# The scale of a gate's weights: one four-column fp32 matmul, summed by the copying activation, in place of four one-column matmuls

## The chip, the core and the metric

The kernel runs on one core of a Trainium2 chip. Five engines work side by side, each through its own instructions in order: TensorE (PE, matmuls; its weight loads are listed as PEld), VectorE (DVE), ScalarE (ACT), GpSimd (POOL) and SyncE (SP, which issues the DMAs). An engine stops at an instruction whose inputs or buffers are not ready, and everything behind that instruction waits with it. The metric is device time in microseconds, the median of repeated runs. In the traces, f32 in a weight's or product's row stands for fp32 or for the 32-bit matmul type that the code calls F32R; a "hi" and a "lo" part are a value rounded to a shorter type and the remainder.

## What is computed

One layer of a hybrid encoder on 1024 tokens of width 1024: RMS norm, one input projection, attention and a gated MLP beside each other, a projection of each, a merge by two sigmoid gates, an output projection, residual and a last RMS norm. The part that matters here is the merge:

```
h = rmsnorm(x, norm_gain)
g_merge = h @ w_in[:, 2816:4864]                     # 2 x 1024 columns
g = sigmoid(g_merge.reshape(B, S, 2, 1024) + b_merge)
y = g[:, :, 0, :] * y_a + g[:, :, 1, :] * y_b
out = rmsnorm(x + y @ w_out, final_gain)
```

## The kernel before

Channels are handled in eight tiles of 128. After attention come these stages: eight projections of the MLP branch (tile `yb`, line 634, PSUM copied to `y` at line 635), then for each of the eight channel tiles a *pair* of gates (`g0` to `g7`), and between them the projections of the attention branch (`y`, lines 806 ff.), then the output projection (`out`).

The two gates of a channel tile are computed together by Strassen's scheme in Winograd's form: the products are named `11`, `21`, `T2`, `T3`, `T1`, `22` and `T4`, in this order, each of four times three matmuls (line 174: hi times hi, line 175: weight hi times data lo, line 176: weight lo times data hi), 84 matmuls in a pair. The weights of a pair are loaded raw (`graw`, lines 811 and 812, two transfers of 512 KB), combined into sums (`s1`, `s2`), and split into an fp16 hi part by ACT (line 682) and a lo part by DVE (line 683), into the tiles `wg..`; three buffers of these exist. The data side are the forms `xf..` of the normalised input, made once by DVE and ACT from `xraw` (lines 112, 118 and 650) around the last `yb` projections; the forms of the attention output (`gf..`, `gk`, from `gat`) are made on the same lines in the same place.

So that the fp16 parts stay in range, the weights of a pair are divided by the root of their mean square. `pair_weights` squares the four raw quarters on ACT, each with a sum per partition into one column of `ss` (line 816, tile `gss`). `unit_scale` then adds the four columns over all partitions by matmuls with a constant matrix (line 671, tile `usg`), copies the result (line 673), and makes the scale on POOL in four small operations (lines 674 to 677, tile `scg`); ACT and DVE need the result of line 675 for the hi and lo parts, and line 677's for the tanh.

Nothing in the source fixes the order on the engines. A scheduler with a time line of its own orders the instructions of each engine, and tiles are taken from pools when it has a buffer free: of the tag `qT` there are four of 8 KB per partition, which hold `gat0`, `gat2`, the `graw` tiles and the `ya` tiles in turn. The order of the steps is asked for by one line:

```
MORDER = "w0 g0 w1 g1 w2 A a0 g2 w3 g3 w4 a1 g4 w5 g5 w6 a2 g6 w7 a3 o g7"
```

`w` is `pair_weights`, `g` the pair of gates, `A` the forms of the attention output, `a` its projections.

Of the kernel before, what the change touches and what calls it, by code (L numbers as in the profile page):

```python
# [12 lines left out]
AF = mybir.ActivationFunctionType  # L13
# [3 lines left out]
P = 128  # L17
# [13 lines left out]
def hybrid_block_kernel(  # L31
# [11 lines left out]
    act, dve, pool, pe = nc.scalar, nc.vector, nc.gpsimd, nc.tensor  # L43
# [24 lines left out]
    def const(shape, name, dt=F32):  # L68
        return sb.tile(shape, dt, tag=name, bufs=1, name=name)
# [4 lines left out]
    def ps_o(name):  # L74
        return ps.tile([P, 512], F32, tag="o", bufs=1, name=name)

    def ps_z(name):
        return ps.tile([P, 512], F32, tag="z", bufs=1, name=name)

    def ps_oz(i, name):  # L80
        return (ps_z if i % 2 else ps_o)(name)
# [13 lines left out]
    mscale = const([P, 1], "mscale")  # L95
# [169 lines left out]
    for h in range(2):  # L265
        pt = ps_o(f"wsum{h}")
# [143 lines left out]
    pt = ps_o("vabT")  # L410
# [4 lines left out]
    pt = ps_z("vmxB")  # L415
# [18 lines left out]
    for t2k in range(4):  # L434
        pt = ps_oz(t2k, f"ktp{t2k}")
# [230 lines left out]
    def unit_scale(ss, n, name):  # L666

        nscale.append(name)
        pt = ps_oz(len(nscale), f"us{name}")
        for i in range(n):  # L670
            pe.matmul(pt[:, 0:1], mscale.broadcast_to([P, P]), ss[:, i:i + 1], start=(i == 0), stop=(i == n - 1))
        sc = sb.tile([P, 2], F32, tag="sc", bufs=3, name=f"sc{name}")
        act.copy(sc[:, 1:2], pt[:, 0:1])  # L673
        pool.tensor_scalar(out=sc[:, 1:2], in0=sc[:, 1:2], scalar1=1.0, scalar2=1e-30, op0=ALU.mult, op1=ALU.add)  # L674
        pool.tensor_tensor(out=sc[:, 0:1], in0=sc[:, 1:2], in1=mhalf[:, 0:1], op=ALU.pow)
        pool.tensor_tensor(out=sc[:, 1:2], in0=sc[:, 1:2], in1=sc[:, 0:1], op=ALU.mult)
        pool.tensor_scalar(out=sc[:, 1:2], in0=sc[:, 1:2], scalar1=gsc[:, 1:2], scalar2=1.0, op0=ALU.mult, op1=ALU.mult)
        return sc
# [130 lines left out]
    def pair_weights(dt):  # L809
        t = t8("qT", 4, f"graw{dt}", F32)  # L810
        nc.sync.dma_start(out=t[:, 0, :], in_=wall[W_TR + 20 + dt])
        nc.sync.dma_start(out=t[:, 1, :], in_=wall[W_TR + 12 + dt])
        a21, a22, a11, a12 = (t[:, k, H(h)] for k in range(2) for h in range(2))
        ss = small(f"gss{dt}", 4)
        for i, t in enumerate((a21, a22, a11, a12)):
            act.activation(junk(f"gsq{dt}{i}"), t, AF.Square, accum_out=ss[:, i:i + 1])
        sc = unit_scale(ss, 4, f"g{dt}")
        return sums(a11, a12, a21, a22, t2(f"s1{dt}"), t2(f"s2{dt}")), sc
# [65 lines left out]
    for step in MORDER.split():  # L884
        i = int(step[1:] or 0)
# [153 lines left out]
```

## Time and profile before

| | |
|---|---|
| median of 3 runs | 735.65 us (735.62 to 738.46) |
| the profiled execution | 736.99 us |
| its span, first to last instruction | 735.2 us |
| PE busy | 714.0 us (97%) |
| DVE busy | 565.9 us (77%) |
| ACT busy | 431.2 us (59%) |
| POOL busy | 110.4 us (15%) |
| mean granted TensorE clock | 0.992 |

The profiled execution is 1.3 us (0.2%) above the median; 1.8 us of it lie outside the span. In rows of a timeline the columns are start, duration (both us), engine, line, operation, output<-input tiles with buffer numbers left out, shape, count, and in brackets the idle time of the engine ahead of it with what ended it. Neighbouring instructions on one engine overlap a little, so their distance is shorter than a duration. The rows of the chain of waits give start, length and what the time was spent on. In the rows of a table by stretches of time, busy time and number of instructions are given for PE, PEld, DVE, ACT and POOL, then the granted TensorE clock (1.00 is full), the share of DMA and GB/s.

### The profile page before, as it was taken

The numbers are of one execution on the slowest core, as the hardware profiler recorded it, in microseconds if no ns is written. First come the engines' busy times: TensorE is split into PE (matmuls) and PEld (weight loads), VectorE is DVE, ScalarE is ACT, GpSimd is POOL, SyncE is SP. The second block draws the span as 40 slices with busy tenths as digits, with TensorE's granted clock in tenths as the row PEclk, the third lists the DMA queues.
The fourth block names the chain that finished last, engine by engine and source line by source line (L and its number), as shares of the span: only waits on it lengthen the run. The fifth ranks groups of instructions, "written<-read, shape, count | busy, mean of one in ns | idle before, by whom it ended". The sixth has DMA issues, their size and how long they took to land.

```text
span 735.2 us, 11836 instructions
## 1 busy us (share of the span) xinstructions
PE 714.0 (97%) x4633; PEld 531.4 (72%) x4633; DVE 565.9 (77%) x822; ACT 431.2 (59%) x770; POOL 110.4 (15%) x101
## 2 busy tenths in 40 slices
PE   8999999998999999999999996999999999999996
PEld 8978888776777788788887883465464556488885
DVE  6556868799797988878789999888887898952223
ACT  6634564685797887777784775654455536621011
POOL 0011223133132232213200003001101110000000
PEclk9999999999999999999999998999999999999999
DMA  8830301054889999998999500130121005440202
GB/s 307 317 129 1 115 16 43 1 122 94 150 157 182 176 180 167 183 170 175 154 245 287 132 30 14 45 129 15 46 98 58 0 1 184 157 146 1 114 30 86
DMA packets 152904, 85.59 MB, mean 116 GB/s; under 512 B 135440, under 2 KB 136080, under 8 KB 152848
## 3 DMA queue, kind: packets, MB, share of 16 engines
q1 hardware_dynamic: 152560, 84.56, 46.6%
q8 instruction: 36, 0.59, 0.3%
q10 hardware_dynamic: 288, 0.28, 0.1%
q14 instruction: 20, 0.16, 0.1%
HBM read 47.07 MB, written 4.19 MB: 70 GB/s over the span
## 4 chain that ended last, share of the span: by engine, by line
PE 83%; DVE 5%; ACT 5%; DMA 5%; issue 1%; POOL 1%; SPq 0%; POOLq 0%; ACTq 0%; DVEq 0%
PE o L576 5%; PE out L175 4%; DMA T<-p 4%; PE out L176 4%; PE out L174 4%; PE s L550 3%; PE s L551 3%; PE g L174 3%; PE g L175 3%; PE g L176 3%; PE gb L488 2%; PE q L174 2%; PE q L175 2%; PE v L175 2%; PE v L174 2%; PE q L176 2%
## 5 line engine op out<-in xcount | busy, mean ns | idle before, releaser
L564 DVE SCALAR_TENSOR_TENSOR p<-P,ri,p 128x1024 f16<-128x1024 f32 x64 | 83.4, 1304 | 26.4 <-ACT p L563 26.3
L557 ACT ACTIVATE P<-s,nm 128x1024 f32<-128x1024 f32 x64 | 71.2, 1113 | 24.2 <-DVE nm L553 20.8
L563 ACT ACTIVATE p<-P,ri 128x1024 f16<-128x1024 f32 x64 | 73.1, 1145 | 15.7 <-DMA T<-p 8.8
L553 DVE TENSOR_REDUCE nm<-s 128x1 f32<-128x1024 f32 x64 | 77.6, 1214 | 3.0 <-PE s L551 2.9
L576 PEld LDWEIGHTS <-vS 128*64 128x64 f16 x1536 | 45.3, 111 | 19.0 <-issue 17.8
L576 PE MATMUL o<-T,vS 128*64 128x128 f16 x1536 | 52.0, 222 | 4.2 <-DMA T<-p 3.8
L118 POOL TENSOR_TENSOR wl<-wraw,wh 128x512 fp32r<-128x512 f32 x24 | 39.9, 1665 | 97.7 <-ACT wh L112 55.6
L550 PE MATMUL s<-kT,qT 128*128 128x512 f32 x128 | 52.9, 413 | 0.0
L551 PE MATMUL s<-kT,qT 128*128 128x512 f32 x128 | 50.9, 397 | 0.0
L911 ACT ACTIVATE sq<-xr 128x1024 f32<-128x1024 f32 x7 | 7.4, 1062 | 65.4 <-DVE xr L969 65.4
L969 DVE TENSOR_TENSOR xr<-out,xr 128x1024 f32<-128x1024 f32 x7 | 8.6, 1224 | 47.6 <-PE out L176 47.5
L674 POOL TENSOR_SCALAR scg<-scg 128x1 f32<-128x1 f32 x8 | 6.5, 807 | 206.7 <-ACT scg L673 206.6
L550 PEld LDWEIGHTS s<-kT,qT 128*128 128x128 f32 x128 | 24.3, 189 | 6.3 <-issue 0.2
L551 PEld LDWEIGHTS s<-kT,qT 128*128 128x128 f32 x128 | 24.3, 190 | 5.4 <-issue 0.2
L112 ACT CAST wh<-wraw 128x512 fp32r<-128x512 f32 x35 | 21.4, 616 | 10.4 <-PE ga L489 3.4
L682 ACT ACTIVATE wg<-graw,scg 128x512 f16<-128x512 f32 x16 | 11.4, 721 | 26.6 <-PE g L176 13.2
L488 PE MATMUL ga<-xh,wh 128*128 128x512 f32 x64 | 26.0, 406 | 0.8 <-DVE ga30w L494 0.5
L488 PE MATMUL u<-xh,wh 128*128 128x512 f32 x64 | 25.8, 402 | 0.0
L488 PE MATMUL gb<-xh,wh 128*128 128x512 f32 x64 | 25.5, 399 | 0.0
L175 PE MATMUL yb<-gml,wh 128*128 128x512 f32 x64 | 25.5, 398 | 0.0
L490 PE MATMUL u<-xh,wl 128*128 128x512 f32 x64 | 25.4, 397 | 0.0
L490 PE MATMUL gb<-xh,wl 128*128 128x512 f32 x64 | 25.4, 396 | 0.0
(554 smaller groups left out, 2143.9 us busy)
## 6 DMA issues: line engine op xcount, KB each, us to landing
wraw<-in_wall_dram SPq DMA_DIRECT2D x59, 256.0 KB, 3.4
graw<-in_wall_dram SPq DMA_DIRECT2D x16, 512.0 KB, 5.8
xraw<-in_xT_dram SPq DMA_DIRECT2D x13, 512.0 KB, 6.4
xn<-in_x_dram SPq DMA_DIRECT2D x8, 512.0 KB, 6.3
wor<-in_wall_dram SPq DMA_DIRECT2D x8, 512.0 KB, 5.1
xr<-in_x_dram SPq DMA_DIRECT2D x8, 512.0 KB, 3.8
out_dram<-xr SPq DMA_DIRECT2D x7, 512.0 KB, 2.6
xraw<-in_xT_dram SPq DMA_DIRECT2D x5, 256.0 KB, 5.5
```

What stands on the lines that cost most here:

```text
L174: pe.matmul(o, ah, bh, start=start, stop=False)
L175: pe.matmul(o, ah, bl, start=False, stop=False)
L176: pe.matmul(o, al, bh, start=False, stop=stop)
L488: pe.matmul(o, wh[:, C(dt % 4)], xh[dt][:, H(h)], start=(dt == 0), stop=False)
L490: pe.matmul(o, wl[:, C(dt % 4)], xh[dt][:, H(h)], start=False, stop=(dt == 7))
L550: pe.matmul(sp[:, H(hf)], qs, kT[:, 2 * v, H(hf)], start=True, stop=False)
L551: pe.matmul(sp[:, H(hf)], qs, kT[:, 2 * v + 1, H(hf)], start=False, stop=True)
L553: dve.tensor_reduce(out=nm, in_=sp, axis=AX.X, op=ALU.max, negate=True)
L557: act.activation(Pt, sp, AF.Exp, bias=nm, accum_out=rsum)
L563: act.activation(hi, Pt, AF.Copy, scale=ri)
L564: dve.scalar_tensor_tensor(out=lo, in0=Pt, scalar=ri, in1=hi, op0=ALU.mult, op1=ALU.subtract)
L576: pe.matmul(ot[64 * h:64 * h + 64, 0:128], vS[:, kt, v, 64 * vl:64 * vl + 64], T[:, h, 8 * p + kt, :], start=(n == 0), stop=(n == len(part ...
```

## The change

Four matmuls of one column, each adding to the same PSUM column, become one matmul of four columns. The copy from PSUM becomes an activation that copies the four sums to an unused place of the same PSUM tile and adds them into the scale tile by its accumulator. The sum is the same; 24 of the 32 matmul instructions of the eight pairs go, and the eight activations each get an instruction that reads the accumulator.

```
 pt = ps_oz(len(nscale), f"us{name}")
-for i in range(n):
-    pe.matmul(pt[:, 0:1], mscale.broadcast_to([P, P]), ss[:, i:i + 1], start=(i == 0), stop=(i == n - 1))
+pe.matmul(pt[:, 0:n], mscale.broadcast_to([P, P]), ss[:, 0:n], start=True, stop=True)
 sc = sb.tile([P, 2], F32, tag="sc", bufs=3, name=f"sc{name}")
-act.copy(sc[:, 1:2], pt[:, 0:1])
+act.activation(pt[:, 8:8 + n], pt[:, 0:n], AF.Copy, accum_out=sc[:, 1:2])
```

The scheduler orders the program anew. Line numbers from 672 on are one lower in the changed kernel (its line 670 is the matmul, 672 the activation, 681 and 682 the hi and lo parts, 815 the squares); the text uses the numbers of before. Names in the rows below carry the pair's number and the product (`wg011` is the weight of pair 0, product 11) and a buffer number.

On ACT, around the first scale, before: the copies of the scales of pairs 0 and 1 stand behind the last `y` copy (`y47<-yb7`), and the first hi parts behind them.

```order
L635 COPY y47_5097<-yb7_5442 128x1024
L112 CAST gk_5829<-gat2_4640 128x1024
L673 COPY scg0_5491<-usg0_5486 128x1
L673 COPY scg1_5645<-usg1_5640 128x1
L112 CAST xfT33_5399<-xraw7_5229 128x512
L682 ACTIVATE wg011_5505<-graw0_5474,scg0_5491 128x512
L682 ACTIVATE wg021_5522<-graw0_5474,scg0_5491 128x512
```

On ACT, the same place after:

```order
L112 CAST gf110_5801<-gat0_2003 128x1024
L635 COPY y47_5097<-yb4_5321 128x1024
L112 CAST xf222_5305<-xraw2_5167 128x512
L672 ACTIVATE usg0_5486,scg0_5488<-usg0_5486 128x4
L112 CAST xfT40_5164<-xraw4_5104 128x512
L112 CAST xfT22_5312<-xraw6_5169 128x512
L112 CAST xfT42_5318<-xraw3_5227 128x512
L112 CAST xfT11_5210<-xraw1_5106 128x512
L112 CAST wp0011_5840<-wraw380_5831 128x256
L635 COPY y47_5097<-yb5_5353 128x1024
L681 ACTIVATE wg011_5502<-graw0_5474,scg0_5488 128x512
```

The scale of pair 0 has moved ahead by three `y` copies and stands in the middle of the making of the forms, and its first hi part stands two `y` copies ahead of the last. The cast `gf110` has moved behind the cast of the last MLP weights and so stands directly ahead of the copy of `yb4` and the cast of `xf222`.

On DVE, the stretch that leads to the first lo part, after; before, `wg011` stood 19 rows further down, behind the last of the forms of product 21.

```order
L118 TENSOR_TENSOR gf111_5802<-gat0_2003,gf110_5801 128x1024
L118 TENSOR_TENSOR xfT22_5312<-xraw6_5169,xfT22_5312 128x512
L118 TENSOR_TENSOR xfT42_5318<-xraw3_5227,xfT42_5318 128x512
L650 TENSOR_TENSOR xraw1_5106<-xraw5_5108,xraw1_5106 128x512
L118 TENSOR_TENSOR xfT11_5210<-xraw1_5106,xfT11_5210 128x512
L118 TENSOR_TENSOR wp0011_5840<-wraw380_5831,wp0011_5840 128x256
L650 TENSOR_TENSOR gat0_2003<-gat0_2003 128x2x512
L682 SCALAR_TENSOR_TENSOR wg011_5502<-graw0_5474,scg0_5488,wg011_5502 128x512
```

The same set of operations up to `wp0011` and the subtraction `gat0` stood there before; the lo part of pair 0 now follows them. Further down, up to the lo part of pair 0's product T4, DVE has three operations fewer ahead of it than before: the last subtraction on `gat2` (line 650), `gk` and `gfT31` (line 118) now stand behind it.

On PE, the scale of pair 2. Before, its four matmuls stood between matmuls of pair 0 (one in product T1, one in 22, two at the end of 22); here the last two:

```order
L176 LDWEIGHTS wg022_5592
L176 MATMUL g022_5595<-xfT13_5392,wg022_5592 128x512
L671 MATMUL usg2_5794<-gss2_5785,mscale_63 128x1 x2
L174 LDWEIGHTS wg0T4_5610
L174 MATMUL g0T4_5613<-xfT40_5164,wg0T4_5610 128x512
```

After, the only one stands between the end of pair 0 and pair 1:

```order
L176 LDWEIGHTS wg0T4_5607
L176 MATMUL g0T4_5610<-xf213_5404,wg0T4_5607 128x512
L670 MATMUL usg2_5788<-gss2_5779,mscale_63 128x4
L174 LDWEIGHTS wg111_5653
L174 MATMUL g111_5656<-xf110_5146,wg111_5653 128x512
```

It has moved behind the last product of pair 0. The buffers moved too: before, the raw weights of pair 2 (`graw2`) were put into the buffer that `gat0` leaves; in the changed program they get the buffer of `graw0`, whose last reader is the lo part of pair 0's product T4 on DVE. The rows of SP stand in the same order in both. The matmuls of the scales of pairs 3 to 7 stood before as three together and one alone (pairs 3, 5 and 7) or as four apart (4 and 6); now each pair has one.

## The prediction

> **What bounds the kernel now.** I read the page first, then who waits for whom on PE, the chain of waits around the longest such wait, and then each engine's instructions in order of time there.
>
> ```profile
> span 735.2 us, 11836 instructions
> PE 714.0 (97%) x4633; PEld 531.4 (72%) x4633; DVE 565.9 (77%) x822; ACT 431.2 (59%) x770; POOL 110.4 (15%) x101
> PE g L174 <- ACT wg L682: 6.2, 1, 6.2
> 443.73 0.94 ACT gk L112
> 444.83 3.56 POOL scg L674
> 448.75 0.57 POOL scg L675
> 449.34 0.73 ACT wg L682
> 450.11 0.61 PE g L174
> 451.15 0.43 PE g L174
> 453.48 0.22 PE g L175
> ```
>
> PE is busy for 97% of the span: an instruction taken out of its row is worth its full time, and so is a wait. The third row is PE's longest wait, 6.2 us ahead of the first gate product; the chain says what it consists of: the scale of pair 0 (3.56 and 0.57 us on POOL), then the first hi part.
>
> ```profile
> 400.00:440.00 40.00, 40.00 (x216) 32.35 (x215) 39.56 (x64) 28.70 (x55) 0.00 (x0) 1.00 0.40 116
> 452.00:453.00 1.00, 1.00 (x4) 0.30 (x2) 1.00 (x2) 0.74 (x2) 0.00 (x0) 0.50 0.00 0
> 453.00:454.00 1.00, 1.00 (x6) 0.45 (x5) 1.00 (x3) 0.00 (x0) 0.00 (x0) 0.94 0.00 0
> 175.00:180.00 5.00, 1.92 (x15) 1.18 (x10) 5.00 (x7) 2.29 (x4) 0.00 (x0) 1.00 0.57 108
> 180.00:185.00 5.00, 5.00 (x54) 3.79 (x54) 5.00 (x6) 2.54 (x7) 2.34 (x1) 0.66 0.13 40
> ```
>
> Two things stand here. From 400 to 440 us DVE has no room either (39.56 of 40 us). And PE's wait costs more than 6.2 us: until 453 the clock is halved, so the first seven matmuls of the product are 0.43 us apart and not 0.22 (the last two rows of the chain), 1.5 us more. A wait of 3.08 us did the same at 175 us.
>
> **The wait that goes, and the one that comes.** Once the scale of pair 0 is computed among the `yb` products, its 6.2 us and the 1.5 us of half clock go. If nothing took their place, pair 0 would start when the `yb` matmuls end, where the scale matmuls stand before (442.5 in the rows below). Its 84 matmuls took 470.35 - 450.11 = 20.24 us with 1.5 of half clock and four scale matmuls of some 0.16, so 18.1 us without (0.216 each). Pair 1 would start at 460.6 and not at 470.35: 9.7 us, the upper end of this term. It will not be reached, because DVE has to finish the forms first. DVE's rows before, with two of ACT's and two of PE's:
>
> ```profile
> 427.63 0.69 DVE L118 TENSOR_TENSOR xf<-xraw,xf 128x512 f16<-128x512 f32 x1
> 432.99 0.42 DVE L118 TENSOR_TENSOR wp<-wraw,wp 128x256 fp32r<-128x256 f32 x1
> 437.35 0.43 DVE L118 TENSOR_TENSOR wp<-wraw,wp 128x256 fp32r<-128x256 f32 x1 [0.41 <-ACT wp L112]
> 447.65 0.69 DVE L650 TENSOR_TENSOR xraw<-xraw 128x512 f32<-128x512 f32 x1
> 450.09 1.41 DVE L683 SCALAR_TENSOR_TENSOR wg<-graw,scg,wg 128x512 f16<-128x512 f32 x2 [1.75 <-ACT wg L682]
> 455.04 1.21 DVE L650 TENSOR_TENSOR gat<-gat 128x1024 f32<-128x1024 f32 x1
> 456.18 1.21 DVE L118 TENSOR_TENSOR gfT<-gat,gfT 128x1024 fp32r<-128x1024 f32 x1
> 462.91 0.75 DVE L683 SCALAR_TENSOR_TENSOR wg0T<-graw,scg,wg0T 128x512 f16<-128x512 f32 x1
> 423.94 1.05 ACT L112 CAST gf<-gat 128x1024 fp32r<-128x1024 f32 x1
> 426.98 0.61 ACT L112 CAST xf<-xraw 128x512 f16<-128x512 f32 x1
> 442.52 1.39 PE L671 MATMUL usg<-gss,mscale 128*128 128x1 f32 x12
> 470.35 0.38 PE L174 MATMUL g<-xf,wg 128*128 128x512 f16 x1
> ```
>
> Between 427.63 and the end of pair 0's last lo part (product T4, 462.91 + 0.75 = 463.66) DVE idles twice, 0.41 and 1.75 us. In the changed order I count the same work to the same point, with these differences.
>
> - Three operations of 1024 elements no longer stand ahead: 3 x 1.13 (the distance of the two in the rows) = -3.4 us.
> - Both idle times go: -2.16 us.
> - The cast `gf` (1.05 us, distance 0.95) moves ahead of the `xf` cast, which ends at 427.59 and now at 428.54; DVE starts that form at 428.6 and not at 427.63: +1.0 us.
> - A new wait: DVE reaches the lo part `wg011` behind `wp` and `gat` at 432.99 + 0.33 + 1.0 + 1.13 = 435.45 (the last result at 435.55), and has to wait for the scale, if POOL only now makes it.
>
> Whether it does is the question of the POOL rows:
>
> ```profile
> L674 POOL TENSOR_SCALAR scg<-scg x8: 191/484/3562, 444.8 to 601.9; 128x1 f32<-128x1 f32 x8
> 468.46 0.71 POOL L674 TENSOR_SCALAR scg<-scg 128x1 f32<-128x1 f32 x1 [16.82 <-ACT scg L673]
> 468.36 0.75 DVE L683 SCALAR_TENSOR_TENSOR wg<-graw,scg,wg 128x512 f16<-128x512 f32 x1
> ```
>
> The same operation on 128 x 1 takes from 0.19 to 3.56 us. The longest began at 444.83 and ended at 448.39, 0.05 us after DVE's last back-to-back operation (447.65 + 0.69 = 448.34); the one at 468.46 ended at 469.17, 0.06 us after a DVE operation with two SBUF inputs (469.11). So I take it that POOL is kept out as long as DVE runs such operations back to back. In the changed program POOL is asked behind the `xf` cast and the new activation (428.5 + 0.34 = 428.9), and DVE has nothing else in its row up to 435.55. Then line 674 (0.27), a gap (0.08), line 675 (0.57), ACT's hi part (0.73) and three hand-overs (0.05 each) follow: DVE starts again at 437.3, +1.75 us. The page "SBUF — State Buffer" of the Trainium skill says under "Who interferes with whom" that a DVE instruction with two SBUF inputs locks out a GpSimd instruction that reads SBUF, for its whole length. The trace agrees in both places (0.05 and 0.06 us after DVE's end); by the rule this term is +1.75 us, without it 0, which is the first rival below.
>
> ACT waits for the scale meanwhile, with two `y` copies behind it; their PSUM banks are asked for again only by pair 0's second and third product, so `yb` does not notice.
>
> Sum for DVE: 463.66 - 3.4 - 2.16 + 1.0 + 1.75 = 460.85.
>
> **What is late next.** The raw weights of pair 2 now need the buffer of `graw0`, so their load waits for just this lo part, and PE stands at pair 2's only scale matmul ahead of pair 1. Before, SP waited for `gfT`:
>
> ```profile
> SPq L811 <- DVE gfT L118: 30.0, 1, 30.0
> 457.45 0.33 SPq L811 DMA_DIRECT2D graw<-in_wall_dram  x1
> graw<-in_wall_dram SPq DMA_DIRECT2D x2, 512.0 KB, 4.5
> DMA to landing us min/median/max: 3.6/5.8/8.7
> 461.07 0.60 ACT L816 ACTIVATE gsq<-graw 128x512 f32<-128x512 f32 x1 [0.74 <-DMA graw<-in_wall_dram]
> L816 ACT ACTIVATION_READ_ACCUMULATOR gsq<-graw x32: 185/187/197, 413.1 to 591.6; 128x1 f32 x32
> L673 ACT COPY scg<-usg x8: 140/150/173, 444.6 to 601.7; 128x1 f32<-128x1 f32 x8
> ```
>
> Issue at 460.9. The first transfer was there 3.6 us after its issue (457.45 to 461.07); with a median of 4.5 for the two the second took 5.4, and it is issued 0.4 later: 466.7. Its two quarters are squared in 0.75 us each (0.60 and 0.19, overlapped): 468.2. Matmul and hand-over 0.2: pair 1 starts at 468.4 and not at 470.35, **-1.95 us**. PE itself gets there earlier: T4's bank is freed by DVE three operations after 460.85, at about 463.8, and 12 matmuls take 2.6 us, so it is done at 466.4 and waits 2.0 us.
>
> **The matmuls taken out.** In pairs 3 to 7 they stand in PE's row and nothing hides them:
>
> ```profile
> 500.89 0.56 PE usg L671 x6
> 506.92 0.28 PE L671 MATMUL usg<-gss,mscale 128*128 128x1 f32 x2
> 507.06 0.38 PE L176 MATMUL g2T<-xf,wg2T 128*128 128x512 f16 x1
> ```
>
> Three together (two passes each) take 0.56 us, one alone 0.14. Pairs 3, 5, 7 lose 0.56 + 0.14 - 0.14 each, pairs 4 and 6 lose 3 x 0.14: 1.68 + 0.84 = **-2.5 us**. Those of pairs 0 to 2 lie inside the first term. Four columns for one I take at the same 0.14: a 512-column matmul takes 0.43 us at half clock, so three columns more cost under 0.01. The new activation is 0.15 us plus 0.19 for its accumulator; the 8 x 0.19 = 1.5 us lie on ACT, which is busy for 59%, and would count in full only if ACT held PE in every pair.
>
> **Sum.** 1.95 + 2.5 = 4.45 us off the profiled execution (736.99, 1.3 above the median), taken off the median: 735.65 - 4.45 = 731.2 us. The measurement can tell about 0.5% (3.7 us) from no change, so this is just beyond it.
>
> **Rivals.**
>
> POOL is not kept out, and the 3.56 us had another cause. Then the scale is ready at 430 and everything from there is 1.75 us earlier: 729.4 us. Against it stand the two ends within 0.06 us of DVE's.
>
> The load comes late. Its landing times go up to 8.7 us. With 8.7 for the second transfer PE waits 2.0 + 3.3 us, and as after 6.2 us the clock is halved, 1.5 more: 736.0. For it speaks only the spread; before, the two went over idle queues, as they will now. A wait of 3 us alone, with the clock halved, gives 733.7.
>
> The clock is halved through pair 0: the slower side. PE has 18.3 us of work in the 24 us up to 466.4 and then waits 2.0: 7.9 us of short waits from about 447.3 on. If the clock falls at the first, the 61 matmuls left need 13.2 us more, of which the 7.9 absorb their part; 5.3 remain, with 1.5 to recover in pair 1: 731.2 + 6.8 = 738.0. It decides from 4.45 us lost. Against it: the halved clock showed only after waits of 3.08 and 6.2 us, and none of these should be over 2.2. The page "TensorE: Matmul & The Clock Gate" of the Trainium skill has the case under "A second HAM failure mode: psum-queue depth-cycling": frequent short idle times between groups of matmuls can switch the clock to and fro. No row here shows it without a long wait.
>
> The stretch is rearranged but PE gains nothing in it, since DVE is its limit: only the 2.5 us remain, 733.1.
>
> **Chances.** The forecast (730.2 to 732.4) 0.47; POOL not kept out 0.17; late load or one halved clock 0.15; nothing gained in pair 0 0.13; clock halved through pair 0, or another wait of that size, 0.08. Faster by over 0.5% (under 732.0): three quarters of the first and all of the second, 0.53. Slower by over 0.5% (over 739.3): the upper part of the last case, 0.05. The rest, 0.42, within 0.5%. The range reaches from a little below the first rival, 728.9, to the late load, 736.0.
>
> **What would show it.** In the changed profile: no wait on PE of 6 us at the first gate product and full clock there; line 674 of pair 0 long, ending with DVE's last operation ahead of the first lo part, and about 1.7 us of idle DVE there; PE waiting some 2 us for the squares at pair 2's scale ahead of pair 1; and 8 scale matmuls of 0.14 us. A short line 674, a wait on PE of over 3 us, or a clock below 0.95 between 445 and 470 us would make it wrong.

## The result and the profile after

The changed kernel takes 730.21 us (median of 6 runs, 729.55 to 731.12); its time is 0.9908 of the kernel before's, 95% interval 0.989 to 0.9925. The profiled execution took 730.20 us against 736.99, and its span is 6.8 us shorter. In that comparison the kernel before took 735.62 to 738.46 us in five runs; a sixth, of 1018.11 us, is left out as a slow one. The three runs shown before lay low: in the three later comparisons the kernel before had medians of 736.96 (14 runs), 737.8 (11) and 737.49 (15).

From the page of the changed kernel, the first line, the busy times, and the longest waits on PE by what they wait for (us in total, times, longest); below them the stretch from 440 to 470 us, before and after:

```profile
span 728.4 us, 11748 instructions
PE 709.3 (97%) x4585; PEld 525.6 (72%) x4585; DVE 565.5 (78%) x822; ACT 432.4 (59%) x778; POOL 124.5 (17%) x101
PE g0T L174 <- DVE gb L697: 2.0, 1, 2.0
PE usg L670 <- ACT gsq L815: 1.1, 1, 1.1
PE g0T L174 <- ACT xf L112: 0.6, 1, 0.6
PE g0T L175 <- DVE xfT L118: 0.5, 1, 0.5
```

```profile
440.00:470.00 30.00, 23.80 (x115) 12.65 (x114) 25.83 (x35) 18.47 (x33) 8.03 (x11) 0.89 0.10 36
```

```profile
440.00:470.00 30.00, 25.62 (x117) 11.87 (x116) 29.92 (x42) 20.62 (x37) 14.31 (x8) 1.00 0.10 36
```

The wait of 6.2 us is gone, and the clock in this stretch is 1.00 where it was 0.89. DVE is busy for 29.92 of the 30 us: it is the limit here, and the waits that are left on PE (2.0, 1.1, 0.5 of them) end with work that stands in its row or behind it. PE has 4.7 us less busy time; the half clock's 1.5 and 24 matmuls of 0.14 make 4.9.

Pair 0's scale, then DVE's rows around it, in the changed kernel (columns as before):

```profile
428.51 0.52 POOL L673 TENSOR_SCALAR scg<-scg 128x1 f32<-128x1 f32 x1 [50.87 <-ACT usg L672]
429.11 0.88 POOL L674 TENSOR_TENSOR scg<-scg,mhalf 128x1 f32<-128x1 f32 x1
...
445.26 3.56 POOL L673 TENSOR_SCALAR scg<-scg 128x1 f32<-128x1 f32 x1 [13.27 <-ACT usg L672]
448.91 5.09 POOL L674 TENSOR_TENSOR scg<-scg,mhalf 128x1 f32<-128x1 f32 x1
```

```profile
428.29 0.69 DVE L118 TENSOR_TENSOR xf<-xraw,xf 128x512 f16<-128x512 f32 x1 [1.08 <-ACT xf L112]
428.90 0.68 DVE L650 TENSOR_TENSOR xraw<-xraw 128x512 f32<-128x512 f32 x1
...
435.74 0.73 DVE L682 SCALAR_TENSOR_TENSOR wg<-graw,scg,wg 128x512 f16<-128x512 f32 x1
...
448.70 0.74 DVE L682 SCALAR_TENSOR_TENSOR wg0T<-graw,scg,wg0T 128x512 f16<-128x512 f32 x1
...
453.51 0.68 DVE L697 TENSOR_TENSOR ga<-g,p1g 128x512 f32<-128x512 f32 x1
...
458.37 0.73 DVE L682 SCALAR_TENSOR_TENSOR wg0T<-graw,scg,wg0T 128x512 f16<-128x512 f32 x1
```

The scale of pair 0 took 0.52 and 0.88 us in its first two operations and was ready at 430 us, though DVE ran without a gap from 428.29 on; the first lo part (435.74) did not wait for it. The scale of pair 1 took 3.56 and 5.09. Pair 0's last lo part ends at 458.37 + 0.73 = 459.10. What follows it, on SP (the second of the two transfers of `graw2`; the first is issued at 459.13), ACT and PE:

```profile
459.51 0.42 SPq L811 DMA_DIRECT2D graw<-in_wall_dram  x1
462.85 0.60 ACT L815 ACTIVATE gsq<-graw 128x512 f32<-128x512 f32 x1 [2.04 <-DMA graw<-in_wall_dram]
463.61 0.60 ACT L815 ACTIVATE gsq<-graw 128x512 f32<-128x512 f32 x1
464.36 0.60 ACT L815 ACTIVATE gsq<-graw 128x512 f32<-128x512 f32 x1
465.89 0.39 PE L670 MATMUL usg<-gss,mscale 128*128 128x4 f32 x2 [1.11 <-ACT gsq L815]
466.13 0.38 PE L174 MATMUL g<-xf,wg 128*128 128x512 f16 x1
```

Pair 1 starts at 466.13 and not at 470.35: 4.2 us of the 6.8. The other 2.6 lie behind it.

### The profile page after: what moved, and what is told of

The parts are those of the page before. It is cut to its first block, busy times and chain, and to the rows that moved or that the text cites. A ratio compares the mean times of both kernels' runs of the same rounds, so it can differ in the third digit from the quotient of the medians.

```text
span 728.4 us, 11748 instructions
## 1 busy us (share of the span) xinstructions
PE 709.3 (97%) x4585; PEld 525.6 (72%) x4585; DVE 565.5 (78%) x822; ACT 432.4 (59%) x778; POOL 124.5 (17%) x101
## 4 chain that ended last, share of the span: by engine, by line
PE 80%; DVE 10%; DMA 5%; ACT 3%; issue 1%; SPq 0%; POOLq 0%; POOL 0%; ACTq 0%
PE o L576 6%; PE out L175 4%; DMA T<-p 4%; PE out L176 4%; PE out L174 4%; PE s L550 3%; PE s L551 3%; PE g L174 3%; PE g L175 2%; PE g L176 2%; PE gb L488 2%; PE q L174 2%; PE q L175 2%; PE v L174 2%; PE v L175 2%; PE q L176 2%
## 5 line engine op out<-in xcount | busy, mean ns | idle before, releaser
L489 PE MATMUL u<-xl,wh 128*128 128x512 f32 x64 | 25.4, 396 | 0.0
```

## Experiments

**One part at a time.** The condition chooses the old or the new four lines by the pair:

```
+if len(nscale) in (4, 5, 6, 7, 8):      # pairs 3 to 7; for the reverse (1, 2, 3)
     pe.matmul(pt[:, 0:n], mscale.broadcast_to([P, P]), ss[:, 0:n], start=True, stop=True)
     act.activation(pt[:, 8:8 + n], pt[:, 0:n], AF.Copy, accum_out=sc[:, 1:2])
+else:
+    for i in range(n):
+        pe.matmul(pt[:, 0:1], mscale.broadcast_to([P, P]), ss[:, i:i + 1], start=(i == 0), stop=(i == n - 1))
+    act.copy(sc[:, 1:2], pt[:, 0:1])
```

New in pairs 3 to 7 alone:

> Pairs 0 to 2 keep the four matmuls and the copy, pairs 3 to 7 have the single matmul and the activation; up to pair 2 every engine has the order of the kernel before. Theory A (the gain has two separate parts, the place of pair 0's scale and the matmuls taken out of PE's row): the 6.2 us wait on PE stays, the 18 scale matmuls fewer give 18 x 0.14 = 2.5 us, so 2.5 us less than the kernel before. Rival B (all comes from the new order at pair 0, and the matmuls taken out only lengthen waits elsewhere): 0 us, within 0.5 us.

Measured: 734.35 us against 736.96, ratio 0.9965 (0.9954 to 0.9976): 2.6 us less. The profiled span is 732.6, also 2.6 less, with the same wait as before on PE:

```profile
PE g L174 <- ACT wg L686: 6.2, 1, 6.2
```

New in pairs 0 to 2 alone:

> The reverse: pairs 0 to 2 have the single matmul and the activation, pairs 3 to 7 the four matmuls; up to pair 2 every engine has the order of the changed kernel. Theory A: pair 1 starts at about 466 us as in the changed kernel, so 4.3 us less than the kernel before, and 2.5 us more than the changed one. Rival B: 6.8 us less, as the changed kernel. Rival C (it is the count of matmuls alone): 9 matmuls fewer, 1.3 us less.

Measured: 733.0 us, ratio 0.9945 (0.9929 to 0.996): 4.0 us less; span 730.9, 4.3 less. Pair 1 starts as in the changed kernel:

```profile
465.85 0.38 PE L672 MATMUL usg<-gss,mscale 128*128 128x4 f32 x2 [1.13 <-ACT gsq L820]
466.09 0.38 PE L174 MATMUL g<-xf,wg 128*128 128x512 f16 x1
```

The two spans give 2.6 + 4.3 = 6.9 of 6.8 us: the gain is two separate parts, and theory A holds. B and C fall.

**The activation and the columns without the rest.** Only the matmul of the changed kernel differs:

```
-pe.matmul(pt[:, 0:n], mscale.broadcast_to([P, P]), ss[:, 0:n], start=True, stop=True)
+for i in range(n):
+    pe.matmul(pt[:, i:i + 1], mscale.broadcast_to([P, P]), ss[:, i:i + 1], start=(i == 0), stop=(i == n - 1))
```

> Four one-column matmuls as in the kernel before, but each into a PSUM column of its own, and the summing activation of the changed kernel behind them. Every engine has the order of the kernel before (one pair of neighbours on DVE changes places). Theory A (neither the activation nor the columns gain anything; the count of matmuls in PE's row and the place of pair 0's scale do): the 6.2 us wait stays and grows by the activation's 0.2 us, so 0 to 0.3 us more than the kernel before. Rival F (adding up in PSUM over four matmuls costs time): 1 us less or more.

Measured: 737.37 against 737.49, ratio 0.9998 (0.9989 to 1.0007), and again a wait of 6.2 us. No change: neither the activation nor the end of the adding in PSUM is worth anything by itself.

**The order without the matmul.** In the kernel before, pair 0's four matmuls are only traced at high priority (None is the highest, 0 changes nothing):

```
+with tc.high_priority(None if name == "g0" else 0):
     for i in range(n):
         pe.matmul(pt[:, 0:1], mscale.broadcast_to([P, P]), ss[:, i:i + 1], start=(i == 0), stop=(i == n - 1))
```

> No single matmul and no activation anywhere: the kernel before, with the four scale matmuls of pair 0 traced at high priority, so that the scheduler puts them among the yb3 and yb4 products and not up to behind yb7; the forms, the first lo parts and the raw weights of pair 2 then stand as in the changed kernel. Theory A (the order at pair 0 makes its part of the gain, whatever computes the scale): no 6.2 us wait, pair 1 starts about 3.9 us earlier than before (4.3 less three matmuls of 0.14 at pair 2's scale), some 0.4 more lost in pair 0 to pair 1's four matmuls at the most: 3.5 to 3.9 us less than before. Rival C (the single matmul itself is needed): within 0.5 us of before.

Measured: 731.33, ratio 0.9927 (0.9913 to 0.9942): by the ratio 5.4 us less, more than A expected. So pair 0's part needs no single matmul. The scheduler gives each of the four a slot of its own, and in the kernel before the last two came behind `yb7`; one instruction has one slot, among the `yb5` products. A expected too little. One reason stands in DVE's row: with the scale among `yb3` and `yb4` this order also lacks DVE's stop of 1.08 us at the `xf` cast (it has one of 0.60 at 444.64), and pair 1 starts at 465.04, 1.1 us earlier than in the changed kernel. In the profiled execution a part of that is lost again. Its rows on PE at pair 2's scale, and the clock (last column but two):

```profile
462.61 0.38 PE L672 MATMUL usg<-gss,mscale 128*128 128x1 f32 x2 [0.37 <-ACT gsq L817]
463.83 0.38 PE L672 MATMUL usg<-gss,mscale 128*128 128x1 f32 x2 [0.84 <-ACT gsq L817]
464.59 0.59 PE L672 MATMUL usg<-gss,mscale 128*128 128x1 f32 x2 [0.37 <-ACT gsq L817]
465.04 0.59 PE L174 MATMUL g<-xf,wg 128*128 128x512 f16 x1
```

```profile
463.00:464.00 1.00, 0.17 (x2) 0.17 (x2) 1.00 (x3) 0.97 (x4) 0.00 (x0) 1.00 0.00 0
464.00:465.00 1.00, 0.63 (x4) 0.54 (x5) 1.00 (x2) 1.00 (x3) 0.00 (x0) 0.70 0.00 0
465.00:466.00 1.00, 1.00 (x4) 0.45 (x5) 1.00 (x3) 0.49 (x3) 0.46 (x2) 0.50 0.00 0
```

Four scale matmuls that each wait for one square hold PE in short waits, none over 0.84 us, and the clock falls to half from 464.4 to 467.8 us. This execution is the slowest of the six (733.03 us at a mean clock of 0.990; three took 730.8 at 0.995); whether the others lost this too is not shown.

**What decides how long POOL's operations take.** A *border* is here the place between two DVE operations that follow each other without idle time, and POOL is *let in* there when its operation, which takes 0.19 us when it need not wait, ends 0.13 us behind it. Four kernels, none of them the layer: DVE runs one operation over and over, POOL is asked for the four operations of the scale. The core of the first, whose blocks differ by `op`, and its expectation:

```
act.activation(j, g[:, 0:4], AF.Copy, accum_out=sc[:, 1:2])
for i in range(n):
    op(i, g)       # e.g. dve.tensor_tensor(out=o[i % 4], in0=g[:, 0:512], in1=B, op=ALU.subtract)
...                # POOL's four operations of the scale on sc
```

> Not the layer: nine blocks by themselves, in each DVE runs 20 operations of 512 elements back to back (12 of 1024 in one block) while POOL is asked, early in the run, for the scale's four operations on 128 x 1. Blocks by DVE's operation: two SBUF inputs in two tiles, in one tile, fp16 out, a mix of these three, 1024 wide, with a scalar operand, five plain and one with a scalar operand, five plain and one with a PSUM input, all with a PSUM input. Theory L (POOL is kept out as long as DVE runs such operations back to back): the first POOL operation takes about 10 us in the first five blocks and ends within 0.1 us of DVE's last operation there, 0.2 us in the last block, and 2 to 3 us where each sixth has a PSUM input. Rival M (it gets in at some border between two operations, as at pair 0 of the changed kernel): 0.2 to 1 us in every block. Rival N (3.56 us, seen twice, is a fixed time after which POOL is let in): 3.6 us in the first five blocks.

The first two POOL operations of the blocks with two tiles, 1024 wide, and PSUM inputs:

```profile
7.12 0.35 POOL L79 TENSOR_SCALAR sctwo<-sctwo 128x1 f32<-128x1 f32 x1 [6.70 <-ACT jtwo L76]
7.56 0.88 POOL L80 TENSOR_TENSOR sctwo<-sctwo,mhalf 128x1 f32<-128x1 f32 x1
...
61.15 0.89 POOL L79 TENSOR_SCALAR scwide<-scwide 128x1 f32<-128x1 f32 x1 [10.73 <-ACT jwide L76]
62.12 1.41 POOL L80 TENSOR_TENSOR scwide<-scwide,mhalf 128x1 f32<-128x1 f32 x1
...
118.11 0.19 POOL L79 TENSOR_SCALAR scpsum<-scpsum 128x1 f32<-128x1 f32 x1 [10.71 <-ACT jpsum L76]
118.39 0.55 POOL L80 TENSOR_TENSOR scpsum<-scpsum,mhalf 128x1 f32<-128x1 f32 x1
```

M holds in every block, L and N fall: POOL gets in at the next border between two DVE operations (with PSUM inputs it waits for none), and is not kept out for a run. That is pair 0 of the changed kernel, but not pair 1. The next kernel put other engines to work beside it:

> Not the layer: the blocks of the first such kernel with other engines at work. DVE runs 24 operations of 512 elements with two SBUF inputs back to back, POOL is asked for the scale's four operations; beside it nothing, or PE with 60 fp16 matmuls, or PE with 60 matmuls of fp32 type, or ACT with 24 casts; then DVE in a chain in place mixed with operations that each wait for a cast of ACT's, and that with fp16 matmuls on PE. Theory P (fp16 matmuls on PE, which run at pair 1's scale and not at pair 0's, make POOL miss borders): 0.35, 0.88, 0.19 and 1.09 us as before with nothing beside and with fp32, over 2 us for the first or second with fp16 matmuls. Rival Q (ACT's casts do): over 2 us in the block with casts. Rival R (neither; it depends on which operations stand in DVE's row): 0.35 and 0.88 in all of the first four blocks.

First and second operation: 0.36 and 0.88 us with nothing beside, 0.44 and 0.88 with either kind of matmul, 0.36 and 0.88 with casts on ACT. The third operation took 0.76 us beside fp16 matmuls and 0.20 in the other three, one border more. The last three blocks tell nothing here, since the scheduler mixed the operations of two of them in DVE's row. P and Q fall, and R, which stood, named no cause. The traces of the layer had a hint: DVE had just stopped where POOL was quick. So POOL was asked at different places of a run:

> Not the layer: five blocks, in each DVE runs two operations and then 21 to 40 of 512 elements with two SBUF inputs back to back; POOL is asked for the scale's four operations behind the 2nd, 5th, 9th, 13th or 21st of them, with 19 still to come. Theory T (POOL gets in at a border only in the first microseconds after DVE's last stop; the longer DVE has run, the more borders it misses): about 0.35 us for the first operation in the first block, over 2 us in the last ones, where it comes in only at the end of the run, after about 10 us. Rival R (it depends on which operations stand in DVE's row, not on how long it has run): 0.35, 0.88, 0.19 and 1.09 us in all blocks.

The first operation of the blocks in which POOL was asked behind the 2nd, 5th, 9th and 21st (the 13th is as the 9th); behind the 5th also the last of the four, and DVE's two rows at the start of that block's run:

```profile
8.59 0.23 POOL L50 TENSOR_SCALAR sck<-sck 128x1 f32<-128x1 f32 x1 [8.17 <-ACT jk L49]
...
24.51 0.23 POOL L50 TENSOR_SCALAR sck<-sck 128x1 f32<-128x1 f32 x1 [13.26 <-ACT jk L49]
...
26.07 1.09 POOL L53 TENSOR_SCALAR sck<-sck,one 128x1 f32<-128x1 f32 x1
...
42.83 11.07 POOL L50 TENSOR_SCALAR sck<-sck 128x1 f32<-128x1 f32 x1 [15.66 <-ACT jk L49]
...
93.46 11.07 POOL L50 TENSOR_SCALAR sck<-sck 128x1 f32<-128x1 f32 x1 [15.39 <-ACT jk L49]
```

```profile
20.26 0.69 DVE L45 TENSOR_TENSOR gok<-b,gok 128x512 f32<-128x512 f32 x1
20.99 2.50 DVE L47 TENSOR_TENSOR o<-gok,b 128x512 f32<-128x512 f32 x4
```

T holds, and sharply: 0.23 us or the whole rest of the run. The stop is a small one: the operation at 20.99 uses the result of the one just before and starts 0.73 us behind it, where the others start 0.60 apart. What counts is when POOL first asks: in the block asked behind the 5th its three other requests came 3.8, 4.8 and 5.1 us after that stop, and were let in too. A last kernel asked for the bound and for what ends it:

> Not the layer: six blocks as in the last such kernel, DVE with 512-element operations of two SBUF inputs back to back, POOL asked with 19 of them still to come. In the first three it is asked behind the 6th, 7th and 8th; in the others behind the 13th, where in the fourth block that 13th operation and the one behind it each use the result of the one just before, so that DVE stops for about 0.1 us; in the fifth the 17th operation has a scalar operand, and in the sixth it has an input from PSUM in place of one from SBUF. Theory T (a stop of DVE, however short, opens the borders for the next 6 to 9 operations; without one POOL stays out): the first operation is short (0.2 to 0.4 us) in some of the first three blocks and in the fourth; in the fifth it waits to the end of the run, about 11 us; in the sixth it gets in at the 17th, after some 2 us. Theory U (the scalar operand too opens a border, as at pair 1 of the changed kernel): some 2 us in the fifth as well. Rival R (not a matter of stops): 11 us in the fourth block as in the fifth.

The first row is the block with POOL asked behind the 6th; then the first operation of the block with the short stop, and the first of the two blocks with a different 17th operation, each with that 17th operation of DVE behind it:

```profile
11.10 11.07 POOL L59 TENSOR_SCALAR scn<-scn 128x1 f32<-128x1 f32 x1 [10.68 <-ACT jn L58]
...
73.34 0.36 POOL L59 TENSOR_SCALAR scdep<-scdep 128x1 f32<-128x1 f32 x1 [10.70 <-ACT jdep L58]
...
94.19 1.44 POOL L59 TENSOR_SCALAR scscal<-scscal 128x1 f32<-128x1 f32 x1 [18.07 <-ACT jscal L58]
...
116.89 1.44 POOL L59 TENSOR_SCALAR scpsum<-scpsum 128x1 f32<-128x1 f32 x1 [10.57 <-ACT jpsum L58]
```

```profile
95.50 0.75 DVE L52 SCALAR_TENSOR_TENSOR oh<-goscal,one,h 128x512 f16<-128x512 f32 x1
...
118.19 0.68 DVE L54 TENSOR_TENSOR o<-pt,gopsum 128x512 f32<-128x512 f32 x1
```

Asked behind the 6th, 4.1 us after DVE's last stop of 0.1 us, POOL is out for the whole run, and so it is behind the 7th and 8th; behind the 5th, 3.5 us after it, it was in at the next border. A stop of 0.1 us just ahead opens the borders again. A scalar operand and a PSUM input each let POOL in at that operation (ends at 95.63 and 118.33, 0.13 and 0.14 us after its start), and then it is out again. T holds in the fourth and the sixth block (0.36 us, and 1.44 for some 2). It misses in the first three, since its bound of 6 to 9 operations was too wide (it lies between 5 and 6 here), and in the fifth, where U holds: 1.44 us and not 11. R falls.

Whether time or the number of operations makes the bound, one place of the layer tells. In the order experiment the scale of pair 1 was asked 3.7 us after a stop of 0.60 us, in DVE's sixth operation, one of them 1024 wide:

```profile
444.64 0.75 DVE L684 SCALAR_TENSOR_TENSOR wg0T<-s,scg,wg0T 128x512 f16<-128x512 f32 x1 [0.60 <-ACT wg0T L683]
...
448.33 4.85 POOL L675 TENSOR_SCALAR scg<-scg 128x1 f32<-128x1 f32 x1 [22.47 <-ACT scg L674]
```

The seventh operation, at 448.91 and 4.3 us after the stop, did not let it in; the seventh of the block asked behind the 5th, 3.6 us after its stop, did. That speaks for time, with one case.

**What limits the stretch now.** If DVE does, work that it does too early is worth moving. The forms of the attention output are issued behind a lo part of pair 0 (`lo16` collects them in order):

```
-dve.scalar_tensor_tensor(out=lo, in0=raw, scalar=sc[:, 0:1], in1=hi, op0=ALU.mult, op1=ALU.subtract)
+lo16.append(dve.scalar_tensor_tensor(out=lo, in0=raw, scalar=sc[:, 0:1], in1=hi, op0=ALU.mult, op1=ALU.subtract))
...
 elif step == "A":
+    with tc.issue_after(lo16[4].ins):
         make_forms(gat, 2, g_tile, GA, ASUB, AHI, ALO)
```

> The changed kernel, with the forms of the attention output issued on DVE only behind the lo part of pair 0's product T1: seven operations of 1024 elements (1.13 us each) that stood between the scale and pair 0's last lo part now stand behind it or behind pair 1's first lo parts, and pair 2's scale matmul moves behind pair 1's first product. Theory A (from the scale's new place on, DVE sets when pair 0 and the load of pair 2's raw weights end): the waits of 2.0, 1.1, 0.6 and 0.5 us on PE in pair 0 and at pair 2's scale go nearly all, pair 1 starts some 4 us earlier, so 3 to 4 us less than the changed kernel, 10 to 11 us less than the kernel before. Rival D (PE's waits there come from the data side's casts on ACT or from the load, not from DVE's row): within 1 us of the changed kernel.

Measured: 726.97 against 737.8, ratio 0.9864 (0.9843 to 0.9885), faster than the changed kernel too (its interval begins at 0.989): about 3.2 us less than 730.21. A holds; its lower end is met. Pair 1 starts 5.8 us earlier than in the changed kernel. Of these 1.1 lie ahead of the first `yb` matmul (385.53 against 386.64), in stages that the edit does not touch, so 4.7 are its own; 1.7 are given back in two new waits in pair 1 (1.28 and 0.46), of which the longer stands behind pair 1's first row here:

```profile
460.34 0.38 PE L174 MATMUL g<-xf,wg 128*128 128x512 f16 x1 [0.42 <-DVE ga L697]
...
473.40 0.39 PE L176 MATMUL g1T<-xf,wg1T 128*128 128x512 f16 x1 [1.28 <-DVE wg1T L682]
```

Two more: pair 0's single matmul at high priority, alone and with the later forms.

> The changed kernel with the scale matmul of pair 0 traced at high priority: it moves from the yb5 products to the yb4 products, the rest of the order as in the changed kernel but for a few casts. Theory A (the scale is in time already; DVE's later work sets the end): 0 to 1 us less than the changed kernel. Rival E (the scale is still late for the first lo part): 1.5 us less or more.

> Both together: the scale matmul of pair 0 among the yb4 products, and the forms of the attention output behind the lo part of pair 0's product T1. Theory A: as with the later forms alone or up to 1 us less, so 10 to 12 us less than the kernel before. Rival D: within 1 us of the changed kernel.

Measured: 729.3 (ratio 0.989, 0.9872 to 0.9909), which the comparison does not tell from the changed kernel, and 727.17 (0.9861, 0.9838 to 0.9883), the same as the later forms alone. The scale was in time; E falls.

## Why the prediction was right or wrong

It said 731.2 us and faster, just beyond what can be told; measured were 730.2. Its sum, however, was 4.45 us, and 6.8 came. That the two times lie so close is in part luck: it took its sum off a median of three that lay 1.3 to 2.1 us under the later ones. Off the time that the ratio of the comparison implies (730.21 / 0.9908 = 737.0) it gives 732.5, outside the 730.2 to 732.4 of its first chance.

- **Matmuls taken out, 2.5 us:** right. Pairs 3 to 7 alone gave 2.6, and four columns cost what one does (a matmul's two passes take 0.28 us in both kernels).
- **The 6.2 us wait and the half clock go, and DVE becomes the limit:** right. DVE is busy for 29.92 of 30 us, and taking work out of its row moved pair 1, counted from the first `yb` matmul, by another 4.7 us.
- **DVE's sum:** three of its four terms right or nearly so. Both old idle times are gone and the three operations stand behind. The `xf` form waits 1.08 us for its cast, but starts only 0.66 us later than before (428.29; forecast +1.0), and one operation of 512 elements more, some 0.6 us, stands behind it, which the sum left out; the two nearly cancel, and DVE reaches the first lo part at 435.74 (forecast 435.45). **The term that was mis-sized is the new wait for POOL: +1.75 us was forecast (its own figures give 1.85, from 435.45 to 437.3), 0 came.** The last lo part ends at 459.10 and not 460.85, 1.75 us earlier.
- **What is late next:** the load of `graw2` does wait for that lo part and is issued right behind it. The second transfer was taken to need 5.4 us; it needed at most 464.36 - 459.51 = 4.85, since the third square waits for nothing. So the first transfer and the four squares set the time, and not the second transfer. That is the other 0.5 us of the 2.3 by which pair 1's start was missed (466.13 for 468.4).
- **PE's wait at pair 2's scale:** 1.1 us and not 2.0; the other 2.0 us stand ahead of T4, for the bank that DVE frees, as the prediction had it in another place.

The step that failed was the reading of the long line 674; the prediction had named a short one at pair 0 as a sign of being wrong, and 0.52 us came. That POOL is kept out by DVE was right in the kernel before, and its end 0.05 us after DVE's last operation too. The failure was to carry it over to a place where DVE had just stopped. In the kernel before, POOL was asked at 444.83, 7.5 us after DVE's last stop ended (437.35); in the changed one at 428.51, 0.2 us after a stop of 1.08 us that the prediction itself had put there as its +1.0. By the last two kernels of that series, a first request 0.4 to 3.5 us after a stop is let in at the next border, and one from 4.1 us on is not. That this is what opened the border at pair 0 follows from these kernels; in the layer itself the stop alone was not taken away.

The same reading explains the scale of pair 1, asked 17 us after that stop: its first operation ends at 448.82, 0.12 us into a lo part, which has a scalar operand, and its second at 454.00, inside an operation with a PSUM input. Nobody waits for it on the path, since pair 1's first hi part comes later.

The Trainium skill, "SBUF — State Buffer", "SBUF: two separate sides", says that of a DVE operation with two SBUF inputs and a GpSimd operation that reads SBUF the one that starts first holds the shared ports for its whole instruction. The traces agree for one instruction: POOL asked at 24.51, inside a DVE operation, and ended at 24.74, 0.13 us behind the start of the next. Who gets the ports between two DVE instructions the page does not say, and the prediction filled that in with "as long as DVE runs".

The first rival, POOL not kept out, had what happens at pair 0's scale right and gave 729.4, as near to the 730.2 as the forecast; its reason, another cause of the 3.56 us, was wrong. It was given 0.17 against 0.47. The rival of the clock halved by short waits did not happen in the changed kernel, where even the 2.0 us wait left it at 1.00. But the argument against it, that the halved clock showed only after waits of 3.08 and 6.2 us, was too narrow: with four scale matmuls and waits of 0.84 us at the most it fell in the profiled execution of the order experiment, and after a wait of 3.08 us it stayed at 1.00 with the later forms. The Trainium skill says in "TensorE: Matmul & The Clock Gate", "A second HAM failure mode: psum-queue depth-cycling", that frequent short idle times can switch the clock. The order experiment's trace agrees as far as it goes; PE did nothing there for 2.7 us but these tiny matmuls, so it may as well count as one long wait.

## What to carry to other kernels

Where a scheduler orders the program, ask of every small instruction on a chain how many slots it needs: four tiny matmuls that add into one result are ready with the last of them, and here that one stood behind the whole MLP projection, after which PE waited 6.2 us; giving the four priority gained at least as much at that place as making them one (5.4 and 4.0 us). When a long duration is put down to another engine's lock, look at what that engine did just before the short cases as well, and carry over the condition, not only the lock. Behind a removed wait stands the engine that is now full, and work on it that nobody needs yet is the next thing to move.

## What the hardware showed that was not expected

- POOL against back-to-back DVE operations with two SBUF inputs: if it first asks up to 3.5 us after a stop of DVE of 0.1 us or more, it is let in at the next border, and its requests right behind that one are too (up to 5.1 us after the stop, in one block); if it first asks 4.1 us after the stop (3.7 in the one case of the layer), it is kept out, up to the full 11.07 us of the rest of the run. A scalar operand or a PSUM input in DVE's row lets it in during that one operation. Why the bound lies there is not shown.
- Matmuls on PE and casts on ACT beside it made next to no difference to its first operation (0.36 to 0.44 us).
- A wait of 2.0 us left PE's clock at 1.00. The same wait of the attention stage, 3.08 to 3.19 us, halved it in eight of the nine profiles of the layer and not in the ninth (3.08 us, the later forms). After four tiny matmuls with three waits of 0.37 to 0.84 us between them, within 2.7 us, it was halved for 3.4 us. But for the last 10 us of a run, every halved stretch in these profiles lasted about 3.4, 6.8 or 10.2 us. So the length of a wait alone does not decide; what does is not shown.
